# The end of a forgetting attention: who splits the query weights, and when

## Chip, cores, metric

The kernel runs on one core of a Trainium2 chip. The metric is device time in microseconds of one execution. All matmuls take float32 operands as pairs of a high and a low part (`F32R` tiles) and add three products (`mm3`), or two where one operand needs no low part; making these pairs ("splitting") is work for ScalarE (the high part, a cast), and VectorE or GpSimd (the low part, a subtraction).

## The reference

One encoder layer on 2048 tokens of width 1024. The part around the change is the forgetting attention (8 heads of 64), its output projection, and then the query projection of a memory attention:

```python
s = jnp.einsum('bhqd,bhkd->bhqk', qb, kb) * scale + c[:, :, start:end, None] - c[:, :, None, :end]
s = jnp.where(kpos[None, :] <= qpos[:, None], s, -jnp.inf)
p = jax.nn.softmax(s, axis=-1)
outs.append(jnp.einsum('bhqk,bhkd->bhqd', p, vb))
...
h = h + jnp.einsum('bsc,cd->bsd', jnp.concatenate([fox, pool], axis=-1), w_out[l])
hn = rmsnorm(h, g_mem_q[l])
mq = rmsnorm(head_split(jnp.einsum('bsd,dc->bsc', hn, w_mem_q[l]), MEM_HEADS, MEM_HEAD_DIM), g_q_mem[l])
...
act = jax.nn.silu(gu[..., :D_FF]) * gu[..., D_FF:]
h = h + jnp.einsum('bsf,fd->bsd', act, w_down[l])
```

## The kernel before

The stages follow each other: the input projection, the pooling branch, the forgetting attention (up to about 938 us of the span), the memory attention, the feed-forward network.

**The attention** is cut into 32 units, one for each head h and block b of 512 queries. A unit has score items (`score_items`, the matmuls at line 689, the row minimum by VectorE at 691 and the exponentials by ScalarE at 702) and value items (`value_items`), one for each chunk of 128 keys: 4, 8, 12 or 16 chunks for b = 0 to 3. For a chunk, TensorE transposes the probabilities into a PSUM tile `tp` (line 767, three buffers), ScalarE casts the high part `ph` (783), VectorE subtracts for the low part `pl` (784, shown at the helper's line 55), and three chunks later (`LAG`) TensorE multiplies both with the values into `acc` (752). In the last diagonal chunk of a unit (q0 = 3) GpSimd first fills a part of `ph` and `pl` with zeros (772). Every eighth chunk that is not at a unit's edge (`SHARE`) goes another way: ScalarE copies it to `pf` (779), GpSimd makes `ph` (780) and `pl` (55), and its matmuls come five chunks later. At the unit's end ScalarE and VectorE add the halves of `acc` into `fo` (728, 729), and GpSimd scales it (735) and stores it to `catT` (737).

**Order.** A loop draws score items until they are 22 (`LEAD`) ahead of the value items, then draws both in turn, and calls `tick()` after each. `later(n, fn)` puts a job off by n ticks. In this block the orders of TensorE, VectorE and ScalarE are as written; GpSimd and SyncE, and what is written behind the block, are placed by the scheduler. The last score matmul is issued at 912.3 us; 22 value items remain, and the output projection follows at 938.5 us.

**Weights made in this time.** `load_w_of` loads the eight 128x512 parts of the output weights through four raw tiles (`wofr`) and splits each with a cast by ScalarE (line 178) and a subtraction by GpSimd (55) into slabs `qs`, `kh`, `kl`, `cb`. At the end of the scores `load_cat(0)` loads the first tile of attention output into `v`, `split_cat` splits it by VectorE (646 and 55), and `load_w_q` loads the query weights: four DMAs of two parts each into `wqr` (822), and eight jobs, each with a gain: `split_gain`, one ScalarE operation (173) and one VectorE operation (174), into the slabs of `hpb`. The jobs of the first two parts are put off by 8 and 10 ticks; the other six are in the list `rest`, which is called in the memory attention after `out_fox` of the first tile (line 1139 on). `out_fox` is the output projection by token tile; `query` and `query_norm` are the query projection, which reads all eight parts.

Of the kernel before, what the change touches and what calls it, by code (L numbers as in the profile page):

```python
# [11 lines left out]
ALU = mybir.AluOpType  # L12
# [4 lines left out]
P = 128  # L17
# [4 lines left out]
H = 8  # L22
# [18 lines left out]
def block_kernel(ctx: ExitStack, tc: tile.TileContext, x, xT, memT, cols, rows, w_qkvf, w_p, w_pool, w_out,  # L41
# [4 lines left out]
    act, dve, pool, pe, sp = nc.scalar, nc.vector, nc.gpsimd, nc.tensor, nc.sync  # L46

    def opened(stack, name, bufs=1, **kw):
        return stack.enter_context(tc.tile_pool(name=name, bufs=bufs, reuse_waits="tile", **kw))

    def f(ap):
        return ap.bitcast(F32)

    def sub_hi(lo, src, hi, eng=None):
        (eng or dve).tensor_tensor(out=lo, in0=src, in1=f(hi), op=ALU.subtract)  # L55
# [24 lines left out]
    g_mix, g_mem_q, g_mem_kv = (colt[:, 8 * i:8 * i + 8] for i in range(3))  # L80
# [91 lines left out]
    def split_gain(hi, lo, raw, gain):  # L172
        act.activation(hi, raw, AF.Copy, scale=gain)
        dve.scalar_tensor_tensor(out=lo, in0=raw, scalar=gain, in1=f(hi), op0=ALU.mult, op1=ALU.subtract)

    def split(hi, lo, raw, gain=None, eng=None):
        if gain is None:
            act.copy(hi, raw)  # L178
            sub_hi(lo, raw, hi, eng)
        else:  # L180
            split_gain(hi, lo, raw, gain)
# [266 lines left out]
    def load_values(h):  # L448
        v = hp.tile([P, NT, P], F32R, tag="v", name="v", bufs=2)
        sp.dma_start(f(v[:]), vd[h])  # L450
        return v

    def load_head(h, pl, queue=sp):
        qs, kh, kl = (slab(n, pl, F32R) for n in range(3))
        cb = slab(3, pl)
        queue.dma_start(f(qs[:]), qkT[h // 4][h % 4])
        for a in range(2):
            queue.dma_start(f(kh[a * DH:(a + 1) * DH, :]), qkT[2 + h // 4][h % 4, :DH])
            queue.dma_start(f(kl[a * DH:(a + 1) * DH, :]), qkT[2 + h // 4][h % 4, DH:])
        queue.dma_start(cb[:], cdr[h].partition_broadcast(P))  # L460
        return qs, kh, kl, cb
# [168 lines left out]
    BACK, SCALE = 22, 12  # L630

    SHARE = 8

    rest = []
    hpb = opened(hps, "hpb")
    wof, wq, cats = {}, {}, {}

# [6 lines left out]
    def split_cat(i):  # L644
        hi, lo, raw = cats[i]
        dve.tensor_copy(hi, raw)
        sub_hi(lo, raw, hi)

    with ExitStack() as c0:
# [7 lines left out]
        def later(n, fn):  # L657
            due.append([n, fn])
# [66 lines left out]
        def finish(unit, acc):  # L725
            h, b = unit["u"]
            fo = tpool.tile([DH, 512], F32, tag="fo", name="fo", bufs=3)
            act.copy(fo[:], acc[DH:, :])
            dve.tensor_tensor(out=fo[:], in0=acc[:DH, :], in1=fo[:], op=ALU.add)
            later(SCALE, lambda: scale(unit, fo))  # L730
# [8 lines left out]
        nchunk = [0]  # L739

        def value_items(unit):
            h, b = unit["u"]
            v = unit["head"][4]
            nk = 4 * (b + 1)
            acc = aps.tile([P, 512], F32, tag="acc", name="acc", bufs=2)
            wait = []
            state = dict(n=0)

            def weighted(j, qa, ph, pl):
                for pm in (ph, pl):  # L750
                    state["n"] += 1
                    pe.matmul(acc[:, qa * P:], lhsT=v[:, j, :], rhs=pm[:, qa * P:], start=state["n"] == 1,
                              stop=state["n"] == 2 * nk)

            def step(flush=False):
                for e_ in list(wait):
                    e_[0] -= 1
                    if e_[0] < 0 or flush:
                        wait.remove(e_)
                        weighted(*e_[1])  # L760

            for j in range(nk):
                q0 = max(0, j - 4 * b)
                qa = min(q0, 2)
                tp = tps.tile([P, 512], F32, tag="tp", name="tp", bufs=3)
                for q in range(q0, 4):
                    pe.transpose(tp[:, q * P:(q + 1) * P], unit["rows"][q][:, j * P:(j + 1) * P], ident[:])  # L767
                ph = tpool.tile([P, 512], F32R, tag="ph", name="ph", bufs=5)
                pl = tpool.tile([P, 512], F32R, tag="pl", name="pl", bufs=5)
                if qa < q0:  # L770
                    for t_ in (ph, pl):
                        pool.memset(f(t_[:, qa * P:q0 * P]), 0.0)
                sl = slice(q0 * P, 512)
                nchunk[0] += 1
                lag = LAG
                if nchunk[0] % SHARE == 0 and 0 < j < nk - 4:
                    lag += 2
                    pf = tpool.tile([P, 512], F32, tag="pf", name="pf", bufs=2)
                    act.copy(pf[:], tp[:])
                    pool.tensor_tensor(out=ph[:], in0=pf[:], in1=ones[:, 0:1].to_broadcast([P, 512]), op=ALU.mult)  # L780
                    sub_hi(pl[:], pf[:], ph[:], pool)
                else:
                    act.copy(ph[:, sl], tp[:, sl])  # L783
                    sub_hi(pl[:, sl], tp[:, sl], ph[:, sl])
                wait.append([lag, (j, qa, ph, pl)])
                step()
                yield True

            def drain():
                step(True)  # L790
                finish(unit, acc)

            later(2, drain)
# [4 lines left out]
        def halves(pl):  # L798

            t_ = [slab(n, pl, F32R) for n in range(4)]  # L800
            return [(t_[n // 4][:, n % 4 * 512:(n % 4 + 1) * 512], t_[2 + n // 4][:, n % 4 * 512:(n % 4 + 1) * 512])
                        for n in range(8)]

        def load_w_of():

            parts = halves(hpa)
            for n, (hi, lo) in enumerate(parts):
                wof[n // 2, n % 2] = hi, lo

                def load(n=n, hi=hi, lo=lo):  # L810
                    g, a = n // 2, n % 2
                    raw = spool.tile([P, 512], F32, tag="s0", name="wofr", bufs=4)
                    sp.dma_start(raw[:], w_out[g * P:(g + 1) * P, a * 512:(a + 1) * 512])
                    later(14, lambda: split(hi, lo, raw[:], eng=pool))

                later(4 + 4 * n, load)

        def load_w_q():
            parts = halves(hpb)
            for c in range(4):  # L820
                raw = spool.tile([P, 1024], F32, tag="s1", name="wqr", bufs=4)
                sp.dma_start(raw[:].rearrange("p (k c) -> p k c", k=2),
                             w_mem_q[c * 2 * P:(c + 1) * 2 * P, :].rearrange("(k p) c -> p k c", p=P))
                for n in range(2 * c, 2 * c + 2):
                    wq[n] = hi, lo = parts[n]
                    job = lambda hi=hi, lo=lo, n=n, v=raw[:, n % 2 * 512:(n % 2 + 1) * 512]: \
                          split(hi, lo, v, g_mem_q[:, n:n + 1])
                    if n < 2:
                        later(8 + 2 * n, job)
                    else:  # L830
                        rest.append(job)

        def all_scores():
            for un in units:
                h, b = un["u"]
                if b == 1 and h + 1 < H:
                    heads[h + 1] = load_head(h + 1, (hpa, hpb)[(h + 1) % 2])
                if b == 3 and h + 1 < H:

                    heads[h + 1] += (load_values(h + 1),)  # L840
                elif h + 1 == H and b == 3:

                    load_w_of()
                un["head"] = heads[h]
                yield from score_items(un)
            load_cat(0)
            later(8, lambda: split_cat(0))
            load_w_q()

        def all_values():  # L850
# [3 lines left out]
        with in_order(EN.DVE, EN.Activation):  # L854
            sg, vg = all_scores(), all_values()
            lead, more = 0, True
            while True:
                if more and lead < LEAD:
                    n = next(sg, None)
                    more = n is not None  # L860
                    lead += more
                else:
                    n = next(vg, None)
# [134 lines left out]
    with ExitStack() as c0:  # L998
# [13 lines left out]
        def load_tile(i):  # L1012

            h1s[i] = h1t(i)
            for c in (i, i + 1):
                if c < NT and c not in cats:
                    load_cat(c)
                    split_cat(c)
# [114 lines left out]
        with in_order(EN.SP):  # L1133
            qd, mqd, qtd, pmd, pts, mod = {}, {}, {}, {}, {}, {}
            for n in range(2):
                load_tile(n)
                for a in range(2):
                    out_fox(n, a)
                if n == 0:
                    for job in rest:  # L1140
                        job()
            qd[0] = query(h1s[0])
            mkv = [pair_place(n)[:].rearrange("p a c -> p (a c)") for n in range(4)]
            mkh, mkl = (t_.rearrange("p (h m) -> p h m", h=MH) for t_ in mkv[:2])
# [2 lines left out]
            for n in range(NT + 1):  # L1147
# [16 lines left out]
                elif n < 4:  # L1164
                    for h in range(2 * n - 4, 2 * n - 2):
                        for a in range(2):
                            wm[h, a] = hi, lo = [w4.tile([P, 512], F32R, name=f"wm{h}{a}{c}") for c in "hl"]
                            raw = hp.tile([P, 512], F32, tag="cm", name="wmr", bufs=3)
# [338 lines left out]
```

## Time and profile before

| | |
|---|---|
| median of 3 runs | 2573.12 us (2572.25 to 2573.79) |
| the profiled execution | 2576.41 us, span 2574.7 us, granted TensorE clock 0.998 |
| TensorE busy | 2535.0 us, 98% of the span |
| VectorE, ScalarE, GpSimd busy | 1700.4, 1248.2, 818.3 us |

A row of the timeline reads: start in us, busy us, engine, line, operation, output<-input, shape, count, and in brackets the idle time ahead of it with what ended it. PE is TensorE, DVE VectorE, ACT ScalarE, POOL GpSimd, SP SyncE. A group row has a count, busy us, mean ns, and idle time with its releaser; a row of one tile has the least, median and longest duration in ns, then the first and last start.

### The profile page before, as it was taken

The numbers are of one execution on the slowest core, as the hardware profiler recorded it, in microseconds if no ns is written. First come the engines' busy times: TensorE is split into PE (matmuls) and PEld (weight loads), VectorE is DVE, ScalarE is ACT, GpSimd is POOL, SyncE is SP. The second block draws the span as 40 slices with busy tenths as digits, with TensorE's granted clock in tenths as the row PEclk, the third lists the DMA queues.
The fourth block names the chain that finished last, engine by engine and source line by source line (L and its number), as shares of the span: only waits on it lengthen the run. The fifth ranks groups of instructions, "written<-read, shape, count | busy, mean of one in ns | idle before, by whom it ended". The sixth has DMA issues, their size and how long they took to land.

```text
span 2574.7 us, 36909 instructions
## 1 busy us (share of the span) xinstructions
PE 2535.0 (98%) x13133; PEld 2179.9 (85%) x13133; DVE 1700.4 (66%) x2933; ACT 1248.2 (48%) x2375; POOL 818.3 (32%) x1087
## 2 busy tenths in 40 slices
PE   8999999999999989999999999999999999999999
PEld 7999989978888878888778888888888888888887
DVE  6444376569999965554777787756766666665554
ACT  6454442158888865444543433334543333333443
POOL 3343240025455443333525445430001222222000
PEclk9999999999999999999999999999999999999999
DMA  6443365346445132222464555447773332334766
GB/s 244 127 127 111 119 217 173 125 137 166 124 113 159 59 127 86 83 82 87 160 221 177 181 180 193 147 159 268 245 261 130 103 122 103 118 108 168 235 207 205
DMA packets 204777, 396.20 MB, mean 154 GB/s; under 512 B 24368, under 2 KB 99888, under 8 KB 193840
## 3 DMA queue, kind: packets, MB, share of 16 engines
q1 hardware_dynamic: 175088, 296.30, 35.9%
q0 software_dynamic: 29504, 97.54, 9.8%
q8 instruction: 103, 1.69, 0.3%
q14 instruction: 82, 0.67, 0.1%
HBM read 268.85 MB, written 124.91 MB: 153 GB/s over the span
## 4 chain that ended last, share of the span: by engine, by line
PE 41%; issue 8%; DVE 1%; POOL 1%; ACT 0%; DMA 0%; POOLq 0%; SPq 0%; DVEq 0%; ACTq 0%
PE bk L62 13%; PE bk L60 13%; PE bk L61 13%; DVE ww L55 0%; POOL out_dram L1400 0%; PE mmps L60 0%; DMA xraw<-hTd 0%; PE mmps L61 0%; PE mmps L62 0%; DVE t L971 0%; PE bk L939 0%; DVE cb L55 0%; ACT ww L178 0%; ACT pm L1073 0%; ACT s3h L178 0%
## 5 line engine op out<-in xcount | busy, mean ns | idle before, releaser
L55 DVE TENSOR_TENSOR ww<-draw,ww 128x512 fp32r<-128x512 f32 x308 | 205.0, 704 | 156.6 <-ACT ww L178 156.4
L178 ACT CAST ww<-draw 128x512 fp32r<-128x512 f32 x308 | 179.4, 620 | 220.1 <-PE bk L62 171.1
L55 DVE TENSOR_TENSOR ww<-graw,ww 128x512 fp32r<-128x512 f32 x220 | 178.4, 817 | 110.2 <-ACT ww L178 109.8
L61 PE MATMUL bk<-ww,ww 128*128 128x512 f32 x616 | 239.8, 389 | 0.0
L60 PE MATMUL bk<-ww,ww 128*128 128x512 f32 x616 | 239.6, 389 | 0.0
L62 PE MATMUL bk<-ww,ww 128*128 128x512 f32 x616 | 239.6, 389 | 0.0
L178 ACT CAST ww<-graw 128x512 fp32r<-128x512 f32 x220 | 136.0, 622 | 181.0 <-PE bk L62 160.9
L55 DVE TENSOR_TENSOR pl<-tp,ph 128x512 fp32r<-128x512 f32 (+3 forms) x296 | 176.9, 599 | 26.2 <-ACT ph L783 24.4
L702 ACT ACTIVATE s<-s,mx 128x1024 f32<-128x1024 f32 (+2 forms) x192 | 173.7, 905 | 4.5 <-DVE mx L696 2.6
L767 PE MATMUL tp<-ident,s 128*128 128x128 f32 x1088 | 171.0, 273 | 4.9 <-DVE pl L55 4.3
L60 PE MATMUL zps<-wh,xhi 128*128 128x386 f32 x512 | 175.7, 343 | 0.1
L61 PE MATMUL zps<-wl,xhi 128*128 128x386 f32 x512 | 173.6, 339 | 0.0
L62 PE MATMUL zps<-wh,xl 128*128 128x386 f32 x512 | 173.2, 338 | 0.0
L783 ACT CAST ph<-tp 128x512 fp32r<-128x512 f32 (+3 forms) x296 | 148.8, 514 | 33.6 <-PE tp L767 28.5
L767 PEld LDWEIGHTS tp<-ident,s 128*128 128x128 f32 x1088 | 132.8, 140 | 32.9 <-DVE pl L55 8.1
L1400 POOL DMA_DIRECT2D out_dram<-o x32 | 17.3, 540 | 382.9 <-DVE o L1397 377.2
L62 PE MATMUL bk<-qs,ww 128*128 128x512 f32 x352 | 137.2, 390 | 1.1 <-DVE ww L55 1.1
L60 PE MATMUL bk<-qs,ww 128*128 128x512 f32 x352 | 137.9, 392 | 0.3 <-ACT s L1319 0.3
L61 PE MATMUL bk<-kh,ww 128*128 128x512 f32 x352 | 137.0, 389 | 0.0
L60 PE MATMUL bk<-kl,ww 128*128 128x512 f32 x352 | 136.9, 389 | 0.0
L61 PE MATMUL bk<-cb,ww 128*128 128x512 f32 x352 | 136.9, 389 | 0.0
L62 PE MATMUL bk<-kl,ww 128*128 128x512 f32 x352 | 136.9, 389 | 0.0
(549 smaller groups left out, 7254.8 us busy)
## 6 DMA issues: line engine op xcount, KB each, us to landing
graw<-in_w_gu_dram SPq DMA_DIRECT2D x44, 1024.0 KB, 5.4
draw<-in_w_down_dram SPq DMA_DIRECT2D x66, 256.0 KB, 4.3
xl<-in_xT_dram SPq DMA_DIRECT2D x64, 256.0 KB, 4.8
qkT<-st SPq DMA_DIRECT2D x64, 256.0 KB, 2.7
wdr<-in_w_down_dram SPq DMA_DIRECT2D x22, 512.0 KB, 4.3
vd<-cb SPq DMA_DIRECT2D x16, 512.0 KB, 3.3
xr<-in_x_dram SPq DMA_DIRECT2D x16, 512.0 KB, 3.4
qs<-qkT SPq DMA_DIRECT2D x8, 1024.0 KB, 6.8
```

Source lines behind the costliest of these rows:

```text
L55: (eng or dve).tensor_tensor(out=lo, in0=src, in1=f(hi), op=ALU.subtract)
L60: pe.matmul(ps, lhsT=sh, rhs=mh, start=first, stop=False, skip_group_check=goes_on)
L61: pe.matmul(ps, lhsT=sh, rhs=ml, start=False, stop=False, skip_group_check=goes_on)
L62: pe.matmul(ps, lhsT=sl, rhs=mh, start=False, stop=last, skip_group_check=goes_on)
L178: act.copy(hi, raw)
L702: act.activation(s[:, sl], s[:, sl], AF.Exp, bias=ng, scale=-1.0, accum_out=l[:, q, g:g + 1])
L767: pe.transpose(tp[:, q * P:(q + 1) * P], unit["rows"][q][:, j * P:(j + 1) * P], ident[:])
L783: act.copy(ph[:, sl], tp[:, sl])
L1400: pool.dma_start(out[rows_, cs], o)
```

## The change

- All eight query-weight splits become jobs of the ticks behind the scores; the list `rest` and its call in the memory attention go. Part n is split after 6 + 2n ticks.
- The odd parts keep `split_gain`. For the even parts GpSimd first multiplies the raw weights by the gain in place, after 4 + 2n ticks; then ScalarE casts and GpSimd subtracts.
- The cast and the subtraction of the first attention tile come after 3 and 5 ticks, in place of both after 8.
- In the last head's units b = 2 and b = 3 no chunk goes to GpSimd. There were two of them in these units.

```diff
-                if nchunk[0] % SHARE == 0 and 0 < j < nk - 4:
+                if nchunk[0] % SHARE == 0 and 0 < j < nk - 4 and not (h == H - 1 and b >= 2):
...
-                    job = lambda hi=hi, lo=lo, n=n, v=raw[:, n % 2 * 512:(n % 2 + 1) * 512]: \
-                          split(hi, lo, v, g_mem_q[:, n:n + 1])
-                    if n < 2:
-                        later(8 + 2 * n, job)
-                    else:
-                        rest.append(job)
+
+                    def job(hi=hi, lo=lo, n=n, v=raw[:, n % 2 * 512:(n % 2 + 1) * 512]):
+                        g = g_mem_q[:, n:n + 1]
+                        if n % 2:
+                            split_gain(hi, lo, v, g)
+                        else:
+                            split(hi, lo, v, eng=pool)
+
+                    if n % 2 == 0:
+
+                        later(4 + 2 * n, lambda n=n, v=raw[:, :512]: pool.tensor_tensor(
+                            out=v, in0=v, in1=g_mem_q[:, n:n + 1].to_broadcast([P, 512]), op=ALU.mult))
+                    later(6 + 2 * n, job)
...
-            later(8, lambda: split_cat(0))
+            later(3, lambda: dve.tensor_copy(cats[0][0], cats[0][2]))
+            later(5, lambda: sub_hi(cats[0][1], cats[0][2], cats[0][0]))
...
-                if n == 0:
-                    for job in rest:
-                        job()
```

More of the change, by code (lines that the diff above doesn't have):

```diff
@@ L632, in block_kernel @@
     SHARE = 8
-    rest = []
     hpb = opened(hps, "hpb")
```

## Prediction

> **What bounds the kernel now.** I read the page first, then the busy time of each engine in stretches around the place of the change, then the waits and the timeline of TensorE there. The page:
>
> ```profile
> span 2574.7 us, 36909 instructions
> ...
> PE 2535.0 (98%) x13133; PEld 2179.9 (85%) x13133; DVE 1700.4 (66%) x2933; ACT 1248.2 (48%) x2375; POOL 818.3 (32%) x1087
> ```
>
> TensorE (PE) bounds the whole: its idle time over the span is 2574.7 - 2535.0 = 39.7 us. The change adds and removes no matmul, so it can win only TensorE idle time near its own place. That place is the end of the forgetting attention, where the last scores are done and 22 chunks of values remain. The stretches (in each row: length, then busy time and count by engine):
>
> ```profile
> 898.00:912.30 14.30, 14.30 (x92) 12.38 (x91) 13.18 (x41) 13.84 (x30) 9.90 (x12) 1.00 0.58 190
> 912.30:925.00 12.70, 10.09 (x62) 7.47 (x60) 9.17 (x19) 11.99 (x25) 8.04 (x10) 1.00 0.27 88
> 925.00:938.50 13.50, 10.65 (x66) 8.55 (x67) 13.18 (x22) 10.52 (x21) 8.95 (x8) 1.00 0.12 23
> ```
>
> The columns are PE, PEld, DVE, ACT, POOL, granted clock, DMA share, GB/s. Ahead of 912.3 TensorE has no idle time (14.30 of 14.30). From 912.3 to 938.5, which I call the tail, it idles 2.61 + 2.85 = 5.46 us. In the tail's first half ScalarE is full (11.99 of 12.70), in its second VectorE (13.18 of 13.50). TensorE's waits, from the waits of the tail and from its timeline:
>
> ```profile
> PE tp L767 <- DVE pl L55: 3.7, 4, 1.8
> PE acc L752 <- POOL pl L55: 1.1, 1, 1.1
> PE tp L767 <- ACT s L702: 0.6, 1, 0.6
> ```
>
> ```profile
> 926.49 0.66 PE L767 MATMUL tp<-ident,s 128*128 128x128 f32 x4 [1.80 <-DVE pl L55]
> ...
> 932.53 0.66 PE L767 MATMUL tp<-ident,s 128*128 128x128 f32 x4 [0.81 <-DVE pl L55]
> ...
> 934.21 0.66 PE L767 MATMUL tp<-ident,s 128*128 128x128 f32 x4 [0.55 <-DVE pl L55]
> ```
>
> The transposes into a tile tp wait until VectorE has taken the low part pl from an older one: 3.7 us of the tail. One wait of 1.1 us is for a chunk whose parts GpSimd made. So 5.46 us, 0.21% of the time, is about the most that can be won. A difference under 0.2% (5.1 us) is what I take as not to be told from no change.
>
> **The change, part by part.** In the kernel before, six of the eight query-weight splits are written after the attention (the list `rest`). The scheduler has in fact put all eight into the tail:
>
> ```profile
> L173 ACT ACTIVATE qs<-wqr,colt x4: 730/736/752, 917.9 to 926.6; 128x512 fp32r<-128x512 f32 x4
> L174 DVE SCALAR_TENSOR_TENSOR kl<-wqr,colt,qs x4: 735/746/752, 918.7 to 929.7; 128x512 fp32r<-128x512 f32 x4
> L173 ACT ACTIVATE kh<-wqr,colt x4: 723/760/772, 927.2 to 932.0; 128x512 fp32r<-128x512 f32 x4
> L174 DVE SCALAR_TENSOR_TENSOR cb<-wqr,colt,kh x4: 743/950/1530, 930.3 to 937.9; 128x512 fp32r<-128x512 f32 x4
> ```
>
> So nothing is taken out of the stage after the attention: the change redistributes the same work within the tail.
>
> *VectorE.* Four of the eight L174 operations go to GpSimd. All eight take 4 x 0.744 + 4 x 1.043 = 7.2 us (means of these groups in the tail), so about 3.6 us go. Two chunks that GpSimd split come back, at the mean of the chunks' low parts:
>
> ```profile
> L55 DVE TENSOR_TENSOR pl<-tp,ph 128x512 fp32r<-128x512 f32 (+3 forms) x23 | 13.7, 615 | 3.8 <-ACT ph L783 3.5
> L174 DVE SCALAR_TENSOR_TENSOR cb<-wqr,colt,kh 128x512 fp32r<-128x512 f32 x4 | 4.2, 1043 | 0.0
> L174 DVE SCALAR_TENSOR_TENSOR kl<-wqr,colt,qs 128x512 fp32r<-128x512 f32 x4 | 3.0, 744 | 0.1
> ```
>
> That is 2 x 0.615 = 1.2 us, so VectorE is relieved of 2.4 us. All four on cb and the last on kl start after 925, in the half where VectorE is full, so most of the relief counts there; its cap is TensorE's idle time of that half, 2.85 us. I take -2.0 us, since chunks then stand behind ScalarE; bounds 0 and -2.85.
>
> *ScalarE.* The number of its operations stays the same. Four L173 (0.74) become casts like that of the output weights (the 0.63 below), 4 x 0.11 = 0.4 us less; the copy pf of the two GpSimd chunks becomes a cast of the same size. The first half of the tail is bound by it, so the 1.14 us wait for GpSimd's chunk goes but is mostly replaced by ScalarE's own pace: I take -0.2 us, bounds 0 and -1.1.
>
> ```profile
> L178 ACT CAST kh<-wofr x4: 630/634/659, 915.7 to 929.9; 128x512 fp32r<-128x512 f32 x4
> L55 POOL TENSOR_TENSOR cb<-wofr,kh x4: 1271/1287/1709, 917.3 to 931.3; 128x512 fp32r<-128x512 f32 x4
> ```
>
> *GpSimd.* It loses two chunks (the rows below) and gets four gain multiplies and four subtractions. A multiply has the form of L780, a tile by a broadcast column: 1.05 us. A subtraction is the row above: 1.29.
>
> ```profile
> L780 POOL TENSOR_TENSOR ph<-pf,ones x2: 1052/1135/1218, 912.6 to 930.1; 128x512 fp32r<-128x512 f32 x2
> L55 POOL TENSOR_TENSOR pl<-pf,ph x2: 1260/1490/1720, 914.8 to 933.0; 128x512 fp32r<-128x512 f32 x2
> ```
>
> In the tail it was busy 8.04 + 8.95 = 17.0 us. Minus 2 x (1.14 + 1.49) = 5.3, plus four subtractions 5.2, one multiply 1.05, and what the multiplies ahead of 912.3 push behind it (a scaling, 1.58 by a row below, and an output-weight subtraction of 1.29): about 20.8 of some 24 us. It fits, with 3 us of room.
>
> *A new wait, ahead of the tail.* In the changed order of GpSimd the first multiply stands behind the last chunk that it splits and ahead of the two zero fills of the next diagonal chunk. That multiply needs its raw weights from the DMA issued at 900.80, which landed 5.2 us after issue:
>
> ```profile
> 900.80 0.38 SPq L822 DMA_DIRECT2D wqr<-in_w_mem_q_dram  x1
> ```
>
> ```profile
> DMA to landing us min/median/max: 5.2/5.2/5.2
> ```
>
> and over all four loads of the query weights:
>
> ```profile
> DMA to landing us min/median/max: 4.2/5.4/6.1
> ```
>
> The first of the two fills as it was, and the matmul that needs them:
>
> ```profile
> 904.76 0.20 POOL L772 MEMSET ph<- 128x128 f32 x1
> ```
>
> ```profile
> 906.51 0.28 PE L752 MATMUL acc<-ph,v 128*128 128x256 f32 x1
> ```
>
> GpSimd would begin at 904.76, stands until 900.80 + 5.2 = 906.0, multiplies until 907.05 and has filled both tiles at about 907.4. TensorE wants them at 906.51 and queues its matmuls in order, so it stops for 0.9 us in a stretch where it had no idle time. Bounds: 0 if the data land at 904.8 (a landing of 4.0; the shortest was 4.2); +1.8 at the longest landing, 6.1 in place of 5.2. Behind it in the queue the first output-weight subtraction frees a raw tile; the next loads on SyncE's queue, one of them query weights, go out later by as much as GpSimd is late, some 2.3 us (907.4 against 904.76 + 2 x 0.2), and their users stand later in the queues by more.
>
> *The first attention tile's split (v, L646 and L55)* moves some ticks earlier, into the first half, where VectorE is idle 12.70 - 9.17 = 3.5 us; its cost, at most two low parts' 1.2 us, is hidden, and without that cover would be paid in full. *The deadlines* hold: the output weights are wanted at 938.52, where their matmuls begin, the query weights only at 952.42 (next rows). GpSimd's last subtraction, the query weights' own, would have to end 14 us after the tail to be late.
>
> ```profile
> 938.52 0.40 PE L60 MATMUL mmps<-qs,v 128*128 128x512 f32 x1
> ```
>
> ```profile
> 952.42 0.50 PE L60 MATMUL mmps<-qs,hT 128*128 128x512 f32 x1 [0.24 <-ACT hT L878]
> ```
>
> **Sum.** +0.9 - 0.2 - 2.0 = -1.3 us. The profiled execution took 2576.41 us (span 2574.7 and 1.7 around it), 3.3 over the median of the runs; it would be 2575.1. From the median, 2573.12 - 1.3 = 2571.8 us. Own range: 0 to +1.8 ahead of the tail, -1.5 to -3.3 in it, so 2569.8 to 2573.4.
>
> **The rivals.** *Slower: VectorE and GpSimd get in each other's way.* The trace has the price:
>
> ```profile
> 910.11 1.58 POOL L735 TENSOR_TENSOR fo<-fo,lbs 64x512 f32<-64x512 f32 x1
> ...
> 926.95 2.16 POOL L735 TENSOR_TENSOR fo<-fo,lbs 64x512 f32<-64x512 f32 x1
> ...
> 930.11 1.22 POOL L780 TENSOR_TENSOR ph<-pf,ones 128x512 fp32r<-128x512 f32 x1
> ```
>
> ```profile
> 926.96 0.73 DVE L174 SCALAR_TENSOR_TENSOR kl<-wqr,colt,qs 128x512 fp32r<-128x512 f32 x1
> ...
> 930.34 1.53 DVE L174 SCALAR_TENSOR_TENSOR cb<-wqr,colt,kh 128x512 fp32r<-128x512 f32 x1
> ```
>
> An L174 that starts inside a GpSimd operation lasts 1.53 in place of 0.75 and ends 0.54 after it; a GpSimd scaling that starts with an L174 lasts 2.16, against 1.58 for the one ahead of the tail. So +0.78 on the one or +0.6 on the other, for each meeting. The Trainium skill's page "SBUF — State Buffer", section "Who interferes with whom", says that a VectorE instruction with two SBUF inputs and a GpSimd instruction that reads SBUF take one port pair in turns, the second to issue blocked until the first is done; by that rule, which these rows bear out, the busier GpSimd of the change meets nearly every such VectorE operation. Six are in the tail after the change (four L174, the cast and subtraction of v). The three in the first half fall into VectorE's idle time there; the three in the second cost 3 x 0.78 = 2.3 us and use up the relief. GpSimd loses another 3 x 0.6 = 1.8 us or more of its 3 us of room, and the zero fills of the last diagonal chunk come last in its queue, so I put 1 us of wait on TensorE for them. Time: +0.9 + 0 + 1.0 = +1.9, 2575.0 us. It decides from the point at which those fills come after TensorE asks. Against it: the splits of the chunks, 22 of VectorE's operations in the tail, have one input in PSUM, and GpSimd's operations beside them kept a median of 1.29.
>
> *No effect: the waits change their owner.* Splits that ScalarE does between the chunks keep it full through the tail, and VectorE's relief goes unused. Only 0.4 us is won there, against 0.9 lost ahead: +0.5, 2573.6 us. For it speaks the first half; against it that ScalarE has 3.0 us idle in the second.
>
> *More.* The raw weights are there in time and VectorE's whole relief and the GpSimd wait are won: 0 - 1.1 - 2.85 = -4.0, 2569.1 us.
>
> **How the numbers follow.** Chances: forecast 0.58, interference 0.19, no effect 0.13, more 0.10. The likeliest is 2571.8. The range runs from 2569.2 to 2575.5: it takes in the forecast's bounds, the no-effect case, the interference case and part of the larger gain. Over 0.2% faster would need all 5.46 us and no wait ahead: 0.03. Over 0.2% slower would need interference at nearly all of GpSimd's operations in the tail (ten times 0.6 is 6 us, less 3 of room, plus 0.9): 0.04. Within 0.2%: 0.93.
>
> **What would show it.** Right: TensorE gets an idle piece of about 0.9 us near 906 behind GpSimd's zero fills; the time from the last score matmul to the first output matmul falls from 26.2 to about 24.0 us; VectorE is no longer full in the second half; stages after it are only shifted. Wrong: no idle piece at 906, or the tail at 26 us with L174 or GpSimd's subtractions well over 0.75 and 1.29 us, or TensorE waiting for a zero fill at the tail's end, or a difference in the stages behind.

## The result, and the profile after

| | before | after |
|---|---|---|
| median | 2572.9 us (2571.68 to 2577.55, 21 runs) | 2576.99 us (2572.39 to 2582.21, 21 runs) |
| profiled execution | 2576.41 us, span 2574.7 | 2575.25 us, span 2573.5 |

The kernel after takes 1.0014 of the time before, with an interval of 1.0008 to 1.0020: some 4 us slower by the medians. The forecast was 2571.8 and the range ended at 2575.5. Its runs also lie further apart, over 9.8 us.

The two spans mislead: the profiled execution of after is shorter by 1.2 us. That comes in the main from a place ahead of the change, where TensorE's granted clock (as a share of full speed) was at half twice in before's execution, for 3.4 us each from 352.1 and from 376.0 us, and not once in after's. The row of the same stretch, first of before, then of after (length, then PE, PEld, DVE, ACT, POOL, granted clock, DMA share, GB/s):

```profile
375.00:386.00 11.00, 11.00 (x80) 11.00 (x81) 9.00 (x17) 4.43 (x8) 8.79 (x15) 0.84 0.86 235
```

```profile
375.00:386.00 11.00, 11.00 (x78) 10.23 (x77) 8.82 (x18) 3.62 (x6) 6.48 (x10) 1.00 0.74 166
```

So the two traces are compared within the attention, from its first score matmul to the first query-weight matmul. Before, these are at 544.40 and 952.42; after:

```profile
540.12 0.28 PE L687 MATMUL sps<-kh,qs 128*128 128x256 f32 x1
...
903.30 0.39 PE L750 MATMUL acc<-ph,v 128*128 128x256 f32 x1 [0.88 <-POOL ph L770]
...
909.21 0.40 PE L687 MATMUL sps<-kl,qs 128*128 128x512 f32 x1
...
917.16 1.09 PE L765 MATMUL tp<-ident,s 128*128 128x128 f32 x8 [1.94 <-DVE pl L55]
...
920.31 0.35 PE L750 MATMUL acc<-pl,v 128*128 128x256 f32 x1 [1.36 <-DVE pl L55]
...
930.94 1.11 PE L765 MATMUL tp<-ident,s 128*128 128x128 f32 x4 [3.84 <-DVE pl L55]
...
939.18 0.40 PE L60 MATMUL mmps<-qs,v 128*128 128x512 f32 x1
...
953.05 0.50 PE L60 MATMUL mmps<-qs,hT 128*128 128x512 f32 x1 [0.24 <-ACT hT L884]
```

The stretch went from 408.0 to 412.9 us, +4.9. Of that 0.9 is the wait for the zero fill at 903.30. The tail, from the last score matmul to the first output matmul, went from 26.2 us (912.30 to 938.52) to 30.0 (909.21 to 939.18): +3.75. The waits of TensorE in the tail, after:

```profile
PE tp L765 <- DVE pl L55: 6.1, 3, 3.8
PE acc L750 <- DVE pl L55: 1.4, 1, 1.4
PE tp L765 <- DVE mx L694: 0.4, 1, 0.4
```

GpSimd no longer appears there, as the change meant, but the waits for VectorE's low parts rose from 3.7 to 7.5 us. The timeline of VectorE says why; three operations are far longer than their kind (0.42 for a cast, 0.69 for a subtraction, 0.74 for an L174):

```profile
914.28 2.36 DVE L852 CAST v<-v 128x512 fp32r<-128x512 f32 x1
...
917.36 2.60 DVE L55 TENSOR_TENSOR v<-v 128x512 fp32r<-128x512 f32 x1
...
925.28 5.00 DVE L174 SCALAR_TENSOR_TENSOR kl<-wqr,colt,qs 128x512 fp32r<-128x512 f32 x1
```

The extra is 1.94, 1.91 and 4.26 us. In the same time GpSimd did this:

```profile
902.06 1.04 POOL L834 TENSOR_TENSOR wqr<-wqr,colt 128x512 f32<-128x512 f32 x1 [1.50 <-DMA wqr<-in_w_mem_q_dram]
903.04 0.20 POOL L770 MEMSET ph<- 128x128 f32 x1
...
911.01 0.57 POOL L735 DMA_DIRECT2D catT<-fo  x1 [0.29 <-POOL fo L733]
911.61 1.05 POOL L834 TENSOR_TENSOR wqr<-wqr,colt 128x512 f32<-128x512 f32 x1
912.61 2.52 POOL L55 TENSOR_TENSOR kl<-wofr,qs 128x512 fp32r<-128x512 f32 x2
915.09 1.25 POOL L55 TENSOR_TENSOR cb<-wofr,kh 128x512 fp32r<-128x512 f32 x1
...
925.43 0.56 POOL L735 DMA_DIRECT2D catT<-fo  x1
926.01 1.29 POOL L55 TENSOR_TENSOR kl<-wqr,qs 128x512 fp32r<-128x512 f32 x1
927.25 1.26 POOL L55 TENSOR_TENSOR cb<-wofr,kh 128x512 fp32r<-128x512 f32 x1
928.47 1.25 POOL L55 TENSOR_TENSOR cb<-wqr,kh 128x512 fp32r<-128x512 f32 x1
```

The cast ends 0.30 us after the subtraction of 915.09, where two zero fills by GpSimd follow; the subtraction of v ends 0.55 after GpSimd's next two subtractions. The L174 of 925.28 begins 0.15 us ahead of the second store, while GpSimd ends the subtraction in front of it. It ends at 930.28, 0.56 after the last of three GpSimd subtractions in a row (928.47 + 1.25 = 929.72); it did not get in after the first, nor after the second. GpSimd's subtractions kept their length. The rest of the loss is in the granted clock:

```profile
928.00:930.00 2.00, 0.00 (x0) 0.00 (x0) 2.00 (x1) 0.00 (x0) 1.72 (x2) 1.00 0.21 66
...
931.00:932.00 1.00, 1.00 (x5) 1.00 (x6) 1.00 (x2) 0.00 (x0) 0.00 (x0) 0.50 0.00 0
932.00:933.00 1.00, 1.00 (x5) 0.70 (x4) 0.37 (x2) 0.91 (x2) 0.00 (x0) 0.50 0.00 0
...
934.00:935.00 1.00, 1.00 (x9) 0.79 (x7) 0.67 (x2) 0.67 (x2) 0.00 (x0) 1.00 0.00 0
```

Near the end of the 3.84 us in which TensorE did nothing its clock fell to 0.50, from 930.3 to 933.7. The two chunks there took 1.76 and 1.38 us (transposes at 930.94, 932.70, 934.08), against 0.90 for the next: 1.3 us more. The waits grew by 2.5 us (5.4 to 7.9); with 1.3 that is about the tail's 3.75.

### The profile page after: what moved, and what is told of

It is laid out like the page before. It is cut to its first block, busy times and chain, and to the rows that moved or that the text cites. A ratio compares the mean times of both kernels' runs of the same rounds, so it can differ in the third digit from the quotient of the medians.

```text
span 2573.5 us, 36911 instructions
## 1 busy us (share of the span) xinstructions
PE 2531.9 (98%) x13133; PEld 2177.7 (85%) x13133; DVE 1704.9 (66%) x2931; ACT 1248.8 (49%) x2375; POOL 820.8 (32%) x1091
## 4 chain that ended last, share of the span: by engine, by line
PE 84%; issue 8%; DVE 3%; ACT 1%; POOL 1%; DMA 1%; POOLq 0%; DVEq 0%; SPq 0%; ACTq 0%
PE bk L62 13%; PE bk L60 13%; PE bk L61 13%; PE sps L687 5%; PE acc L750 5%; PE tp L765 4%; PE zps L60 4%; PE zps L61 4%; PE zps L62 4%; PE mmps L60 3%; PE mmps L62 3%; PE mmps L61 3%; PE oo L62 1%; PE oo L60 1%; PE oo L61 1%
```

## Experiments

Each ratio is to the kernel before, timed beside it on the same chip. "A meeting" is a VectorE operation with its operands in SBUF that starts while GpSimd works.

**The kernel after, unaltered, and the two halves of the change.** First, is it the same again:

> The changed kernel once more, unaltered, for a second profile and beside the others on one chip. Two theories of its loss. P (port): a VectorE operation with two inputs in SBUF, or the cast of v, that starts inside a run of GpSimd operations that follow without a pause waits for the whole run, not for one operation. Then some of the six such operations of the tail (four L174, the cast and the subtraction of v) again last over 2 us, not necessarily the same ones, TensorE waits behind them, and the time is 2574 to 2580 us with a wide spread. Q (queue): VectorE's operation at 925.28 lasted 5.0 us by an accident of that one execution. Then all six are under 1.6 us, and the tail is near 26 us.

2577.54 us, ratio 1.0016 (1.0007 to 1.0025). The same three operations are long: 2.41, 2.59 and 5.00 us; TensorE waits 1.23 for the zero fill and 2.00, 1.35 and 3.85 for VectorE. So the loss is of the kernel, not of one run. The tail is 31.5 us here, 1.6 longer, with nearly the same waits: the clock stayed at half for 6.8 us in place of 3.4.

```profile
932.00:934.00 2.00, 2.00 (x9) 1.70 (x9) 1.37 (x3) 1.07 (x2) 0.00 (x0) 0.50 0.00 0
934.00:936.00 2.00, 2.00 (x10) 1.70 (x8) 1.61 (x3) 0.72 (x2) 0.00 (x0) 0.50 0.00 0
936.00:938.00 2.00, 2.00 (x9) 1.66 (x8) 0.69 (x1) 1.14 (x3) 0.48 (x1) 0.57 0.00 0
```

Then only the first hunk of the diff on the kernel before:

```diff
+                if nchunk[0] % SHARE == 0 and 0 < j < nk - 4 and not (h == H - 1 and b >= 2):
```

> The kernel before, with only one part of the change: no chunk of the last head's last two units goes to GpSimd; the query weights and the first tile of v as before. If the loss comes from the query weights on GpSimd: VectorE gets 2 x 0.6 us more and TensorE loses its 1.1 us wait for GpSimd, and the time stays within 1.5 us of before, on either side. If taking the chunks from GpSimd is what costs (VectorE full in the second half): +2 us or more.

2571.82 us, ratio 0.9995 (0.9987 to 1.0004). No operation of VectorE on the weights or v is over 1.79 us, the wait of 1.14 us for GpSimd's chunk is gone, and the tail is 25.4 us. This part does no harm.

Then the whole change, but with all query-weight parts split by ScalarE and VectorE, at the same ticks (GpSimd's multiplies, not shown, go too):

```diff
-                        if n % 2:
-                            split_gain(hi, lo, v, g)
-                        else:
-                            split(hi, lo, v, eng=pool)
...
+                        split_gain(hi, lo, v, g)
```

> The changed kernel with one part undone: the even parts of the query weights are split by ScalarE and VectorE like the odd ones, at the same ticks, so that GpSimd has no query weights. VectorE then has eight L174 in the tail in place of four. P: GpSimd's runs are short again, no VectorE operation lasts over 2 us, and although VectorE has four operations more the time falls back to that of before, within 1.5 us, and the 0.9 us wait of TensorE on a zero fill goes. A count of VectorE's work alone would have it 2 to 3 us slower than the changed kernel.

2572.54 us, ratio 0.9999 (0.9990 to 1.0008). The loss is gone, and so is the wait for the zero fill; the longest L174 takes 1.93, though VectorE has four more of them. So the loss hangs on the half of the weights that GpSimd took.

**Without VectorE's second SBUF operand.** The odd parts' L174 reads its subtrahend in PSUM, a score tile that lies there (`last_ps`, kept by lines not shown), so the low parts are not the right ones:

```diff
-                            split_gain(hi, lo, v, g)
+                            act.activation(hi, v, AF.Copy, scale=g)
+                            dve.scalar_tensor_tensor(out=lo, in0=v, scalar=g, in1=last_ps[0][:], op0=ALU.mult,
+                                                     op1=ALU.subtract)
```

> The changed kernel, but the four VectorE operations for the odd parts take their second tile from PSUM (the last score tile) in place of the high part in SBUF; so the low parts of the odd query weights are not the right ones. Everything else, GpSimd's work and order included, is the same. P: the four last 0.75 us each, whatever GpSimd does; only the cast and subtraction of v can still be long; the tail falls by about 4 us against the changed kernel and the time to 2572 to 2574 us. Q or any cause in the queues: the same long operations as in the changed kernel, and no gain.

2574.36 us, ratio 1.0005 (0.9997 to 1.0014), above the 2572 to 2574 expected. The L174s are short (0.74), but another operation met GpSimd's run:

```profile
915.63 5.51 DVE L857 CAST v<-v 128x512 fp32r<-128x512 f32 x1
```

```profile
921.66 1.97 PE L768 MATMUL tp<-ident,s 128*128 128x128 f32 x8 [5.09 <-DVE pl L55]
```

The cast stood through the two zero fills inside GpSimd's run, to 0.3 us after the run's last subtraction. A cast has only one SBUF operand, so it is not the second operand alone. Freed of one meeting, the next operation in line pays.

**The first part back to VectorE.** Part 0 is split by ScalarE and VectorE, with no multiply ahead of the zero fills:

```diff
-                        if n % 2:
+                        if n % 2 or n == 0:
...
-                    if n % 2 == 0:
+                    if n % 2 == 0 and n:
```

> The changed kernel, but the first part of the query weights is split by ScalarE and VectorE, so that no multiply of GpSimd stands ahead of the zero fills near 904. My front term: TensorE's idle piece of 0.9 to 1.2 us there goes and the time falls by about 1 us if nothing else moves. P: VectorE gets a fifth L174, and GpSimd's runs change, so the tail can move by several us either way; the piece at 904 is the test, not the time.

2577.76 us, ratio 1.0013 (1.0004 to 1.0021). The wait of 0.9 us near 904 is gone, so that term was read rightly; but the cast of v now takes 5.44 us and TensorE waits 5.02 in one piece. Where the blow falls depends on shifts of a microsecond.

**All meetings removed.** The operand in PSUM as above, and v's cast by ScalarE, its subtraction by GpSimd:

```diff
-            later(3, lambda: dve.tensor_copy(cats[0][0], cats[0][2]))
-            later(5, lambda: sub_hi(cats[0][1], cats[0][2], cats[0][0]))
+            later(3, lambda: act.copy(cats[0][0], cats[0][2]))
+            later(5, lambda: sub_hi(cats[0][1], cats[0][2], cats[0][0], pool))
```

> Like the run with the PSUM input (the low parts of the odd query weights are not the right ones), and the first tile of v is cast by ScalarE and subtracted by GpSimd, so that no VectorE operation of the tail can meet GpSimd at all. GpSimd gets one subtraction more, ScalarE one cast more. P: no VectorE operation of the tail over 0.8 us, the tail at 24 to 25 us, the wait of about 1 us on the zero fill stays, and the time is 2571 to 2572.5 us: what my sum forecast for the change. If the loss had another part: 2574 us or more.

2571.58 us, ratio 0.9991 (0.9982 to 0.9999): 2.1 under the kernel before beside it (2573.65), where the sum in the prediction had -1.3. No VectorE operation of the tail is over 0.9 us, and the tail is 23.5 us where the prediction had 24.0. So the total of the sum's terms was about right without the meetings, though here v's split has left VectorE too and the interval is wide (-0.3 to -4.6 us).

**What one meeting costs, and when it costs the whole run.** Four small programs apart from the attention: GpSimd makes up to eight subtractions of 128x512 in a row, and VectorE starts one operation inside them. Each program ran once.

> A kernel that computes nothing of the layer (it copies x to the output) and measures the meeting by itself: in fourteen trials GpSimd starts a run of 1.29 us subtractions and VectorE, 0.6 us later, one operation. A to D: the two-input operation of L174's form against runs of 1, 2, 4 and 8. E: a two-input subtraction, F: a cast, G: a subtraction with one input from PSUM, each against 4. H: GpSimd alternates subtraction and multiply, I: subtraction and zero fill. J: four VectorE operations in a row against 4. K: VectorE alternates PSUM and SBUF inputs. L: a run of multiplies. M, N: runs whose operations each wait for the one before. Theory P1 (one operation): VectorE waits for the running GpSimd operation alone, so 1.3 to 1.5 us in A to F whatever the run's length. Theory P2 (the whole run): 1.4 us in A, then 1.25 us more for each further operation, 10 us in D; G 0.7 us; in I it gets in at the first zero fill, in M and N perhaps at the first pause.

```profile
22.52 1.25 DVE L78 SCALAR_TENSOR_TENSOR xoD<-ta,colt,hi 128x512 fp32r<-128x512 f32 x1
34.55 1.31 DVE L55 TENSOR_TENSOR xoE<-ta,hi 128x512 fp32r<-128x512 f32 x1
41.75 1.05 DVE L84 CAST xoF<-ta 128x512 fp32r<-128x512 f32 x1
48.68 0.68 DVE L55 TENSOR_TENSOR xoG<-z,hi 128x512 fp32r<-128x512 f32 x1
```

With GpSimd's run of eight (D) the multiply-subtract takes 1.25, as with one; the two-operand subtraction (E) takes 1.31 and the cast (F) 1.05. With an operand in PSUM (G) nothing is lost: 0.68. So in this program VectorE gets in after one operation, at the price of 0.5 to 0.6 us, and the 5.00 us of the attention is not explained.

> The second kernel that computes nothing of the layer. The first showed one VectorE operation waiting for one GpSimd operation alone, where it came 0.6 us into the first of a run; in the changed kernel it waited for up to four. Here GpSimd's runs are of six subtractions, and VectorE's operation comes after 1 to 5 one-input operations of 0.6 us (A to E: 0.6, 1.2, 1.8, 2.4, 3.0 us into the run); F is a cast at 1.8; G to K add a busy ScalarE, a busy TensorE, both, and DMA; L has a zero fill in the run. P3: it gets in behind the first operation of a run, but later in a run, where GpSimd's operations follow without a pause, it waits for the run's end: 1.3 us in A, some 5 us in C, 4 us in E. P4: other engines' traffic makes the difference: A to E all 0.7 to 1.4 us, G to K up to 7 us. Neither: all under 1.4 us.

All trials gave 0.74 to 1.59 us: neither the moment of arrival, nor a cast, busy neighbours or a zero fill inside the run made a long one. A miss for both theories.

> The third kernel that computes nothing of the layer, with GpSimd's runs made as in the attention: each of six subtractions reads a tile that ScalarE has just cast (A, B) and a tile that a DMA has just loaded (C to L), so that each has waits of its own, fulfilled before its turn. VectorE's operation comes 0.6 us (A, C, E), 1.2 us (J), 1.8 us (B, D, F, I, K) or 3.0 us (L) into the run; G and H have a multiply and a DMA store by GpSimd ahead of the run; I has two zero fills in it; in J the cast reads and writes one tile. P5: waits that are fulfilled ahead let GpSimd's next operation take its turn before VectorE: 3 to 7 us in some of C to L, 1.3 us in A. P6: all under 1.6 us as before; then what keeps VectorE out for a whole run in the attention is not in the form of the two engines' operations.

Ten of twelve gave 1.03 to 1.52 us. The two others, G and H, were the ones with a store issued by GpSimd ahead of its run:

```profile
65.83 7.87 DVE L78 SCALAR_TENSOR_TENSOR xoG<-ta,colt,hi 128x512 fp32r<-128x512 f32 x1
...
77.95 6.87 DVE L84 CAST xoH<-ta 128x512 fp32r<-128x512 f32 x1
```

In the attention, too, each long operation waited on a run behind a store to `catT` (911.01 and 925.43 above; 6.4 us behind it for the subtraction of v). The next program varies the store alone:

> A small program of twelve trials, A to L, apart from the attention: in each GpSimd makes a multiply and then six subtractions of two operands in SBUF, one behind the other, and VectorE starts one operation of 128x512 some 1.5 to 4 us into them. Between the multiply and the subtractions stands a store that GpSimd issues (B, C, D, E, G, H, I, J, L), a store that SyncE issues (F), or a zero fill and no store (A, K). VectorE's operation is the multiply-subtract of line 174's form in A, B, D (started later), F, G (started earlier), J and L (whose subtractions each wait for one semaphore, not two); a cast of one SBUF operand in C, E (with zero fills inside GpSimd's run) and K; a subtraction of two SBUF operands in H; a subtraction with one operand in PSUM in I. In J GpSimd pauses for some 3 us between the store and its run. Theory S (a store issued by GpSimd ahead of an unbroken run makes VectorE wait for the end of the whole run): B, C, D, G, H and L 4 to 8 us each, E about the same or until the zero fill, A, F and K 1.0 to 1.6 us, I 0.7 us; J tells whether a pause clears it (1.3 us) or not (5 us or more). Rival T (what decides is only when VectorE's operation starts against GpSimd's, the store being no part of it): long and short ones are mixed, with long ones in A, F or K as well.

```profile
9.17 1.16 DVE L78 SCALAR_TENSOR_TENSOR xoA<-ta,colt,hi 128x512 fp32r<-128x512 f32 x1
20.45 7.93 DVE L78 SCALAR_TENSOR_TENSOR xoB<-ta,colt,hi 128x512 fp32r<-128x512 f32 x1
32.65 6.88 DVE L84 CAST xoC<-ta 128x512 fp32r<-128x512 f32 x1
...
66.34 0.74 DVE L78 SCALAR_TENSOR_TENSOR xoF<-ta,colt,hi 128x512 fp32r<-128x512 f32 x1
...
100.57 0.68 DVE L55 TENSOR_TENSOR xoI<-z,hi 128x512 fp32r<-128x512 f32 x1
115.45 1.77 DVE L78 SCALAR_TENSOR_TENSOR xoJ<-ta,colt,hi 128x512 fp32r<-128x512 f32 x1
128.56 0.90 DVE L84 CAST xoK<-ta 128x512 fp32r<-128x512 f32 x1
```

All seven trials with GpSimd's store, no pause and operands in SBUF (B, C, D, E, G, H, L) took 5.93 to 8.32 us, to 0.3 to 0.6 us after the end of the run; the zero fills inside E's run released nothing, unlike those at 916.29 in the kernel after. Without a store (A, K), or with the store issued by SyncE (F), it was 0.74 to 1.16; with an operand in PSUM (I) 0.68; with a pause between store and run (J) 1.77.

**The same in the attention.** The changed kernel, with only the two stores moved to SyncE:

```diff
-            pool.dma_start(catT[b][h * DH:(h + 1) * DH, :], fo[:])
+            (sp if h == H - 1 and b in (1, 2) else pool).dma_start(catT[b][h * DH:(h + 1) * DH, :], fo[:])
```

> The kernel after with one difference: the two stores of the attention's output (catT) that GpSimd issues at 911.01 and 925.43 us are issued by SyncE; GpSimd's multiplies, casts of v and query weights' parts are as in the kernel after. Theory S (a store issued by GpSimd ahead of an unbroken run makes VectorE wait for the whole run): the cast of v, its subtraction and the multiply-subtract at 925.28, 2.36, 2.60 and 5.00 us in the kernel after, last 1.6 us or less; TensorE's waits of 1.94, 1.36 and 3.84 us for VectorE's parts shrink to under 1 us each, and the time is 2571 to 2573.5 us. Rival T (the run itself does it, store or no store): the same three operations stay at 1.9 to 5 us, and the time is 2575 to 2578 us, that of the kernel after.

2572.68 us (2571.73 to 2574.46), ratio 0.9997 (0.9988 to 1.0006). The loss is gone, and the runs lie within 2.7 us. The three operations, then GpSimd's beside the last two:

```profile
916.25 1.92 DVE L852 CAST v<-v 128x512 fp32r<-128x512 f32 x1
918.88 1.38 DVE L55 TENSOR_TENSOR v<-v 128x512 fp32r<-128x512 f32 x1
...
926.80 1.48 DVE L174 SCALAR_TENSOR_TENSOR kl<-wqr,colt,qs 128x512 fp32r<-128x512 f32 x1
```

```profile
918.43 1.28 POOL L55 TENSOR_TENSOR cb<-wofr,kh 128x512 fp32r<-128x512 f32 x1 [0.55 <-ACT kh L178]
919.67 1.73 POOL L55 TENSOR_TENSOR kl<-wqr,qs 128x512 fp32r<-128x512 f32 x1
...
926.40 1.33 POOL L55 TENSOR_TENSOR kl<-wqr,qs 128x512 fp32r<-128x512 f32 x1
928.16 1.28 POOL L55 TENSOR_TENSOR cb<-wofr,kh 128x512 fp32r<-128x512 f32 x1 [0.43 <-ACT kh L178]
```

```profile
905.25 0.39 PE L750 MATMUL acc<-ph,v 128*128 128x256 f32 x1 [0.93 <-POOL ph L770]
...
911.17 0.40 PE L687 MATMUL sps<-kl,qs 128*128 128x512 f32 x1
...
935.90 0.40 PE L60 MATMUL mmps<-qs,v 128*128 128x512 f32 x1
```

The subtraction of v tells the theories apart: it ended at 920.26, 0.55 after GpSimd's first subtraction, while GpSimd went on without a pause, its next one drawn out to 1.73. The L174, 1.48 in place of 5.00, doesn't: GpSimd's run itself stopped for 0.43 us behind the operation it met. The cast, 1.92, is above the 1.6 expected, and one of TensorE's waits for VectorE, 1.49, above the 1. The tail is 24.7 us, 1.5 shorter than before, and the wait for the zero fill 0.93 remains: together -0.6, and the medians differ by -0.6, within the noise.

**Versions without meetings.** On the kernel before, the share condition, and all eight parts split by ScalarE and VectorE, spread over the tail:

```diff
-                    if n < 2:
-                        later(8 + 2 * n, job)
-                    else:
-                        rest.append(job)
+                    later((12, 16, 20, 26, 26, 27, 27, 28)[n], lambda hi=hi, lo=lo, n=n, v=raw[:, n % 2 * 512:(n % 2 + 1) * 512]:
+                          split(hi, lo, v, g_mem_q[:, n:n + 1]))
```

> A version made from the finding: no chunk of the last two units and no query weights for GpSimd; three of the eight parts split in the tail (after 12, 16 and 20 ticks), the other five behind its last chunk (after 26 to 28 ticks), where ScalarE and VectorE wait for the first output matmuls; v as before the change. P and the count of VectorE's work agree: the tail falls to 22.5 to 24 us from 26.2, and the output matmuls behind it wait no longer than before: 2569 to 2571 us. If the five parts hold up the first output tile's addition: no gain.

2570.55 us, ratio 0.9988 (0.9979 to 0.9997): faster than both kernels. What it wins in the tail (23.0 us) it gives back in part at the output projection, where TensorE waits 2.13 us for the split of v at 940.06, against 1.12 at that place before.

On the kernel after, the odd parts at tick 26, behind the chunks, and v by ScalarE and GpSimd:

```diff
-                    later(6 + 2 * n, job)
+                    later(26 if n % 2 else 6 + 2 * n, job)
```

> A version that keeps GpSimd's half of the query weights: even parts as changed, the odd parts behind the last chunk (after 26 ticks) where GpSimd is idle, and the first tile of v by ScalarE and GpSimd; no chunk of the last two units for GpSimd. No VectorE operation of the tail meets GpSimd. P: tail 22.5 to 24 us, the 0.7 to 1.2 us wait on a zero fill near 904 stays: 2569.5 to 2571.5 us, as the spread version or a little better. If GpSimd's load itself costs: 2573 us or more.

2569.98 us, ratio 0.9989 (0.9980 to 0.9998), also faster than both, with a tail of 22.5 us, though TensorE still waits 1.08 us at 904.55 and 1.44 at 940.04. Taking the wait at 904 away as well, by giving part 0 to ScalarE and VectorE at tick 26:

> The version that shares without meeting, and its first part also by ScalarE and VectorE behind the last chunk, so that GpSimd has no multiply ahead of the zero fills near 904 and VectorE has five parts behind the tail. Front term of the prediction: TensorE's idle piece of about 1 us there goes; the tail as in the shared version, 22.5 to 24 us; 2569 to 2570.5 us. If the five parts delay the first output tile: the gain is lost behind the tail.

2571.57 us, ratio 0.9994 (0.9985 to 1.0003). The wait went, but another zero fill held TensorE for 1.76 us at 920.35, the tail was 23.0 us, and the wait for v was 2.13 again: nothing was won by it.

## Why the prediction was wrong

*The wait ahead of the tail* (+0.9): right in place, cause and size, 0.88 us in one run and 1.23 in the other, behind a multiply of 1.04 that waited 1.50 us for its DMA in the first (in the second the profile puts its 1.85 us down to a matmul).

*GpSimd has room, and the deadlines hold*: right. It waited 6.17 us for ScalarE near the tail's end, no fill of the last chunk came late, and the stages behind took no longer (1620.5 us from the first query-weight matmul to the end of the span, 1622.3 before).

*ScalarE's term* (-0.2) has no run of its own. With the chunks alone taken from GpSimd the tail was 0.8 us shorter, which speaks against the 1.14 us wait being mostly replaced.

*VectorE's relief* (-2.0): wrong, and this is the step that decided. The sum counted the work that leaves VectorE and gave what stays its length alone; meetings with GpSimd had no term in it, only a price in a rival. Four operations did go, but one of the four that stayed took 5.00 us. With the meetings removed the whole change measured -2.1, and with the stores alone moved the tail was 1.5 shorter than before; so the relief is there, and the meetings ate it. An L174 well over 0.75 us was among the signs of being wrong that the prediction named.

*The split of v is hidden in VectorE's idle time of the first half*: wrong. At 0.42 + 0.69 us it would have been; at 2.36 + 2.60 it held up the low parts queued behind it, and TensorE waited 1.94 and 1.36 us.

*The interference rival* had the right mechanism and sign, and two wrong terms. The price, 0.78 for a meeting, came from an L174 that got in after one GpSimd operation; the meetings of the changed kernel cost 1.9 to 4.3 us, since VectorE stood until GpSimd's run ended. Of its six operations three met GpSimd, two of them in the first half, where it let them vanish in idle time; and it put its last microsecond on zero fills that never came late. The mean share of idle time in a half says nothing on whether one long operation in an engine's order is covered. The Trainium skill, "SBUF — State Buffer", section "Who interferes with whom", has the second engine to issue blocked until the first is done with its instruction; the measured times of at most 1.59 us in the small programs without a store agree, the 5.00 and 7.93 us behind one do not, and there the measurement decides. No end of the range was drawn from the whole run, which the order of GpSimd's instructions showed: three subtractions, 3.8 us.

*The clock* was in no term. One idle piece of 3.84 us halved it for 3.4 us in one run and for 6.8 in the other, which made 1.3 and about 2.9 us; the slowest of after's runs have a lower mean clock (0.996 at 2582.21 us, 0.999 at 2572.39), but what made their spread was not traced run by run. Shorter pieces can do it too. In the kernel before the clock was at half for 3.4 us after waits of 2.24, 1.92 and 2.31 us, from 352.1, 376.0 and 1253.2; the waits of the tail, up to 1.80, left it alone. A wait of 2.31 us near 1250 is in both kernels, and only before's clock fell behind it (before, then after):

```profile
1253.00:1256.60 3.60, 3.60 (x11) 2.83 (x10) 1.17 (x2) 1.72 (x3) 3.15 (x5) 0.53 0.38 152
```

```profile
1253.00:1256.60 3.60, 3.60 (x17) 2.96 (x16) 1.05 (x2) 1.69 (x4) 3.07 (x5) 1.00 0.39 154
```

The Trainium skill, "TensorE: Matmul & The Clock Gate", section "What's actually happening", has a half clock after an idle window of about 3.4 us that runs freely. The trace agrees on the window: the first three half-clock stretches of before are 3.413 us long and start 23.9 and 877.2 us apart, 7 and 257 times that. On the idle time the measurement decides: 1.92 us was enough where it fell so.

Two slips of the working change nothing here: its rows have two L174 on kl behind 925 (926.96 and 929.68), not one, and its sum for a loss over 0.2%, 6 - 3 + 0.9 = 3.9 us, does not reach the 5.1 that it set.

The difference, 0.14%, lies within the 0.2% given the chance of 0.93; the time lies 1.5 us outside the range.

Open: why a store matters. In two places VectorE got in after one operation behind a store, the L174 at 930.34 before and one at 928.12 with the first part back (1.94 us); what differs there was not found. The same happened nine times in the feed-forward network of the kernel before (2.26 us at 1355.87, for example), where GpSimd's second operation began 0.07 to 0.08 us after the end of the first. That GpSimd's store holds something shared until it pauses fits these nine and trial J, and is an argument, not shown. Nor is it known why zero fills ended the cast's wait in the kernel after, but not in E nor in the version with the operand in PSUM.

## What to carry to other kernels

Before work is moved to an idle engine, ask which operations of the other engines will run beside it and price them by the longest unbroken run, not by one operation; a meeting that the trace shows once gives a lower bound. Look at who issues the stores among that work: moved to another queue, two stores were worth the whole loss here. And where TensorE is at 98%, one wait of 2 to 4 us can cost more than the same time in short ones, because the clock can fall to half behind it.

## What was not expected of the hardware

A store issued by GpSimd ahead of an unbroken run of its subtractions makes a VectorE operation on SBUF operands wait for the end of the whole run (5.9 to 8.3 us for a run of 7.4), a cast of one operand included; without the store, or with it issued by SyncE (one trial), such an operation takes 0.74 to 1.59 us in the small programs, and with an operand in PSUM 0.68. These are single runs of small programs, and in the layer's kernels not every store did it.

TensorE's clock fell to half for 3.4 us behind idle pieces of 1.92 to 2.31 us, in some executions and not in others.
